# Down projections of a macaron block: 16 of 22 blocks by seven half-size products, weight sums by adding DMAs

## The chip, the cores and the metric

The kernel runs on one core of one Trainium2 chip. Times are device microseconds of one execution, the median of several runs. The core has a tensor engine (PE, whose weight loads are shown apart as PEld), a vector engine (DVE), a scalar engine (ACT), GpSimd (POOL) and a sync engine (SP). DMAs are issued from queues; in this kernel weights are loaded from SP's queue, and POOL's queue carries gains and some constants.

## The reference, cut to what matters

One layer of a hybrid block on 512 tokens with 1024 channels: a half-step SwiGLU FFN, a token mixer (attention and mLSTM), and a second half-step FFN. The change touches the down projections of the two FFNs only.

```python
D_MODEL, SEQ = 1024, 512
D_FF = ((8 * D_MODEL // 3 + 127) // 128) * 128      # 2816, 22 blocks of 128

def swiglu(x, w_gate, w_up, w_down):
    return (jax.nn.silu(x @ w_gate) * (x @ w_up)) @ w_down

f = swiglu(rmsnorm(x, ffn1_pre_g[l]), ffn1_w_gate[l], ffn1_w_up[l], ffn1_w_down[l])
x = x + 0.5 * rmsnorm(f, ffn1_post_g[l])
...
f = swiglu(rmsnorm(x, ffn2_pre_g[l]), ffn2_w_gate[l], ffn2_w_up[l], ffn2_w_down[l])
x = x + 0.5 * rmsnorm(f, ffn2_post_g[l])
```

All is in float32.

## The kernel before

**Arithmetic.** Each float32 operand is split in a high part (a cast to float32r on ACT) and a low part (the difference, on DVE). A product is three passes: high x high, low x high, high x low. So every weight block and every activation block needs a cast on ACT and a subtraction on DVE (called a low) before PE can use it.

**The down projection** is (512 tokens x 2816) x (2816 x 1024). Its result stands in all eight PSUM banks: `accs[t][b]`, four token tiles t by two column halves b. A *plain* block is one 128-row slice of the weights: 4 x 2 x 3 = 24 matmuls of 128x512 in `step` (L230). Of the 22 blocks, 12 go by seven half-size products (the Winograd form of Strassen's scheme): tokens, rows and columns are halved, and seven products of a quarter of the size do the work of eight. Class `Down` does this. Its rows are cut in three thirds g = 0, 1, 2 of two blocks in each half, and `STEPS` lists the steps as product and third: "20" is product 2 of third 0. One step is 12 matmuls (`product`, L510). Products 1, 2, 3 take a weight block as it lies; 5, 6, 7, 4 take sums of weight blocks, and 5, 6, 7, 3 take sums of activation blocks. Steps p and q are plain blocks (`FILL`), p for the first half of the tokens and q for the second, put in where others need time. `middle` combines accumulators once a product's last third is done.

**How a step is made ready.** `fetch` issues its load on SP into one of six buffers (`room`: three of tag "wf", three of tag "bf"); `sums` makes the sums on DVE, weights into T (in the place of the FFN's input hTh) and activations into S (in the place of hTl); `cast` runs on ACT, `low` on DVE. In the loop of `run`, with step n on PE, loads go out 5 steps ahead, sums and casts 2 ahead, lows 1 ahead. All instructions of this part go through `Order` (`do`), which keeps each engine to the order of the calls, so the order in `run` is the order in the queues of PE, ACT, DVE, SP and POOL.

**Around it.** The first steps are prepared and begun inside the last unit of the gate and up projections (`seven`, a generator `ahead` that is advanced there). After the steps, `down` does the remaining plain blocks 15 to 21: three of them at once, the last four (`KEEP`) held, so that the banks end one after the other and `PostNorm` can take them up. `late` adds an accumulator that is left over. `load_gains` issues two gain rows (second FFN: one) from POOL's queue at the start of the stage.

Of the kernel before, what the change touches and what calls it, by code (L numbers as in the profile page):

```python
# [16 lines left out]
P = 128  # L17
T = 512
# [21 lines left out]
def tile_hybrid_block(ctx: ExitStack, tc: tile.TileContext, a: dict):  # L40
# [42 lines left out]
    def load_w(src, name, n=1024, after=()):  # L83
        wf = act.tile([P, WMAX], F32, tag="wf", bufs=3, name=f"wf_{name}")[:, :n]
        nc.sync.dma_start(wf, src)
        with ExitStack() as st:
            for i in after:
                st.enter_context(tc.issue_after(i))
            wh = wpool.tile([P, WMAX], F32R, tag="wh", bufs=5, name=f"wh_{name}")[:, :n]
            nc.scalar.copy(wh, wf)  # L90
            wl = wpool.tile([P, WMAX], F32R, tag="wl", bufs=5, name=f"wl_{name}")[:, :n]
            nc.vector.tensor_tensor(wl, wf, wh.bitcast(F32), op=ALU.subtract)  # L92
        return wh, wl
# [58 lines left out]
    class PostNorm:  # L152
        def __init__(self, t, g, where, name, half=False):
            self.t, self.g, self.name, self.half = t, g, f"p{name}{t}", half
            self.fg = scratch(f"fg_{name}{t}", *where)
            self.ss = small.tile([P, 2], F32, tag="sp", name=f"sp_{name}{t}")

        def bank(self, acc, b):
# [3 lines left out]
            nc.vector.tensor_tensor(self.fg[:, BANKS[b]], acc[b], self.g[:, BANKS[b]], op=ALU.mult)  # L162
# [37 lines left out]
    def down(n, chunk_src, get_x, post, finish, todo, name, accs=None, first=0, late=lambda: None):  # L200
        pins = []
        held = []
        accs = accs or [pair(f"acc_{name}{t}") for t in range(NT)]
        for kk in range(first, n):
            xh, xl = get_x(kk)
            wh, wl = load_w(chunk_src(kk), f"{name}d{kk}")
            if kk < n - KEEP:
                for t in range(NT):
                    for b in range(2):
                        step(accs[t][b], xh, xl, wh, wl, t, b, kk == 0, False)  # L210
                    if kk == first and t == 1:
                        late()
# [71 lines left out]
    def seven(do, fs, wgu, x, low, scr, aT, name, ahead):  # L284
# [76 lines left out]
        for i in range(len(fs)):  # L361
# [33 lines left out]
            if w:  # L395
# [8 lines left out]
    HALF = 6  # L404
    FILL = (12, 13, 14)
    STEPS = "20 21 10 50 60 11 51 61 12 52 62 22 p0 p1 70 30 p2 71 31 72 32 40 41 42 q0 q1 q2".split()
    LOADS = {"1": ((0, 0),), "2": ((1, 0),), "5": ((0, 1),), "6": ((1, 1),), "7": ((0, 0),), "3": ((1, 1),),
             "4": ((1, 0),)}
# [4 lines left out]
    class Down:  # L413
        after = FILL[-1] + 1

        def __init__(self, do, wdq, wd, aT, scr, name):
            self.do, self.wdq, self.wd, self.aT, self.scr, self.name = do, wdq, wd, aT, scr, name
            self.xp, self.src, self.x, self.w, self.wf = None, {}, {}, {}, {}
            self.accs = [[None, None] for _ in range(NT)]
            self.n = 0  # L420

        def tt(self, out, p, q, op):
            self.do("vector", "tensor_tensor", out, p, q, op=op)

# [7 lines left out]

        def room(self, n):
# [5 lines left out]
        def fetch(self, s):  # L439
            if s[0] in "pq":  # L440
                t = self.room(f"B{s}_{self.name}").rearrange("p a b -> p (a b)")
                self.do("sync", "dma_start", t, self.wd[FILL[int(s[1])]])
                self.src[s] = self.aT[:, FILL[int(s[1])], None, slice(0, H) if s[0] == "p" else slice(H, T)], halves(t, T)
            for k, j in LOADS.get(s[0], ()):
                t = self.room(f"B{k}{j}_{self.name}{s}")
                self.do("sync", "dma_start", t, halves(self.wdq[int(s[1]), k, j], T))
                self.wf[s[1], k, j] = t

        def sums(self, s, early=False):
            k, g = s[0], int(s[1])  # L450
            if k in "pq":
                return
            A, B = (lambda i, j: self.A(i, j, g)), (lambda i, j: self.wf[s[1], i, j])
            x = A(*{"1": (0, 0), "2": (0, 1), "4": (1, 1)}.get(k, (0, 0)))
            w = B(*{"1": (0, 0), "2": (1, 0), "3": (1, 1)}[k]) if k in "123" else None
            if k in "64":
                w = self.T[:, 2 * g:2 * g + 2, :]
            if early:
                w = self.scr.tile([P, 2, Q], F32, tag="cd", bufs=1, name=f"t1_{self.name}")
                x = self.scr.tile([P, 2, Q], F32, tag="ab", bufs=1, name=f"s1_{self.name}")[:, :, :H]  # L460
            elif k in "57":
                x, w = halves(self.S[:, 7, :], H), self.T[:, 6:8, :]
            if k == "5":
                self.t1, self.s1 = w, x
                self.tt(w, B(0, 1), B(0, 0), SUB)
                self.tt(x, A(1, 0), A(1, 1), ADD)
            elif k == "6":
                x = halves(self.S[:, g, :], H)
                self.tt(w, B(1, 1), self.t1, SUB)
                self.tt(x, self.s1, A(0, 0), SUB)  # L470
            elif k == "7":
                self.tt(w, self.T[:, 2 * g:2 * g + 2, :], B(0, 0), SUB)
                self.tt(x, A(0, 0), A(1, 0), SUB)
            elif k == "3":
                x = work.tile([P, 2, H], F32, tag="s4", bufs=1, name=f"s4_{self.name}{g}")
                self.tt(x, A(0, 1), halves(self.S[:, g, :], H), SUB)
            elif k == "4":
                self.tt(w, B(1, 0), w, SUB)
            self.src[s] = x, w

        def cast(self, s, which):
# [4 lines left out]
            self.do("scalar", "copy", halves(hl[0], v.shape[2]), v)  # L486
            (self.w if which == "w" else self.x)[s] = hl

        def low(self, s, which):
            v = self.src[s][which == "w"]  # L490
            h, l = (halves(y, v.shape[2]) for y in (self.w if which == "w" else self.x)[s])
            self.tt(l, v, h.bitcast(F32), SUB)
# [20 lines left out]
        def middle(self, s):  # L513
            q1, p5 = self.S[:, 3:5, :], self.S[:, 5:7, :]
            for i in range(2):
                if s == "12":
                    self.do("scalar", "copy", q1[:, i, :], self.out["1"][i])
                elif s == "52":
                    self.do("scalar", "copy", p5[:, i, :], self.out["5"][i])
                elif s == "62":  # L520
                    self.tt(self.out["6"][i], self.out["6"][i], q1[:, i, :], ADD)
                elif s == "72":
                    self.tt(self.out["1"][i], self.out["7"][i], p5[:, i, :], ADD)
            if s == "62":
# [3 lines left out]
        def late(self):  # L528
            for i in range(2):
                self.tt(self.out["2"][i], self.out["2"][i], self.S[:, 3 + i, :], ADD)  # L530

        def run(self):
            s0, s1, s2, s3, s4 = STEPS[:5]
            self.fetch(s0)
# [4 lines left out]
            self.fetch(s1)  # L539
            self.fetch(s2)  # L540
            self.fetch(s3)
# [3 lines left out]
            self.sums(s3, True)  # L545
# [10 lines left out]
            self.fetch(s4)  # L556
            self.cast(s3, "w")
            yield
            self.cast(s3, "x")
            self.low(s3, "w")  # L560
            self.low(s3, "x")
            self.product(s1)
            self.sums(s4)
            yield
            self.fetch(STEPS[5])
            for x in "wx":
                self.cast(s4, x)
            self.product(s2)
            self.fetch(STEPS[6])
            self.fetch(STEPS[7])  # L570
            for n in range(3, len(STEPS)):
                if n + 5 < len(STEPS):
                    self.fetch(STEPS[n + 5])
                if n + 2 < len(STEPS):
                    self.sums(STEPS[n + 2])
                    for x in "wx":
                        self.cast(STEPS[n + 2], x)
                if n + 1 < len(STEPS):
                    for x in "wx":
                        self.low(STEPS[n + 1], x)  # L580
# [3 lines left out]
    def ffn(pool, todo, first_w, hT, wgu, wdq, wd, post, finish, name, begin=None, pins=(), aT=None):  # L584
# [54 lines left out]
        pins = down(NF, lambda kk: wd[kk], get_x, post, finish, todo, name, d.accs, d.after, d.late)  # L639
# [4 lines left out]
    with new_pool("ffn_a") as fa:  # L644
# [112 lines left out]
        def post1(t):  # L757
            if t == 2:
                hT.extend(new_hT("mx"))
            return PostNorm(t, gains[0], tbuf[t % 2], "f1", True)  # L760
# [640 lines left out]
    with new_pool("ffn_b") as fb:  # L1401
        def post3(t):
            return PostNorm(t, g_post2[0], [(work, "tmp"), (work, "tmp2")][t % 2], "f2", True)
# [43 lines left out]
def _layout(inp):  # L1447
# [11 lines left out]
    for i, n in ((1, "ffn1"), (2, "ffn2")):  # L1459
# [3 lines left out]
        r[f"wdq{i}"] = wd[:12].reshape(2, 3, 2, P, 2, 512).transpose(1, 0, 4, 3, 2, 5).reshape(3, 2, 2, P, 1024)  # L1463
# [51 lines left out]
```

## Time and profile before

| | |
|---|---|
| median of 3 runs | 1348.43 us (1348.35 to 1348.59) |
| the profiled execution | 1348.25 us |
| its span, first to last instruction | 1346.4 us |
| DVE busy | 998.9 us |
| ACT busy | 627.4 us |
| granted TensorE clock | 0.999 |

The first down projection stands at about 238 to 347 us, the second at about 1224 to 1340. A name such as `wh_a` ends in the FFN (a or b); B is a loaded weight block, T and S the sums, `acca` to `accd` pairs of banks, and wh/wl, xh/xl the high and low parts. A row of a timeline has the start, the length, engine, line, operation, output <- inputs, and how many are merged; in square brackets the idle time before it and who ended it. A row of the DMA issues has a count, the size and the median time to landing. A window row has the stretch, its length, and the busy time of PE, PEld, DVE, ACT and POOL with the number of instructions, then the granted clock, the share of the DMA engines, and GB/s.

### The profile page before, as it was taken

The numbers are of one execution on the slowest core, as the hardware profiler recorded it, in microseconds if no ns is written. First come the engines' busy times: TensorE is split into PE (matmuls) and PEld (weight loads), VectorE is DVE, ScalarE is ACT, GpSimd is POOL, SyncE is SP. The second block draws the span as 40 slices with busy tenths as digits, with TensorE's granted clock in tenths as the row PEclk, the third lists the DMA queues.
The fourth block names the chain that finished last, engine by engine and source line by source line (L and its number), as shares of the span: only waits on it lengthen the run. The fifth ranks groups of instructions, "written<-read, shape, count | busy, mean of one in ns | idle before, by whom it ended". The sixth has DMA issues, their size and how long they took to land.

```text
span 1346.4 us, 20568 instructions
## 1 busy us (share of the span) xinstructions
PE 1336.1 (99%) x8247; PEld 1200.1 (89%) x8247; DVE 998.9 (74%) x1511; ACT 627.4 (47%) x1010; POOL 37.1 (3%) x64
## 2 busy tenths in 40 slices
PE   9999999999999999999999999999999999999998
PEld 8899999878998888888888889999888999998786
DVE  7799898996755557475756776766379798997983
ACT  5444444555643544534544444344264444444552
POOL 1000000000300000000000000000010000000000
PEclk9999999999999999999999999999999999999999
DMA  5333333654333422422222212335313233335441
GB/s 197 95 101 110 108 97 110 234 174 152 128 101 122 141 79 94 152 68 78 80 78 78 78 48 78 103 102 196 133 57 102 94 110 108 97 110 202 172 143 62
DMA packets 42719, 153.95 MB, mean 114 GB/s; under 512 B 4836, under 2 KB 4844, under 8 KB 42368
## 3 DMA queue, kind: packets, MB, share of 16 engines
q1 hardware_dynamic: 39456, 140.56, 31.5%
q0 software_dynamic: 3152, 12.08, 2.7%
q8 instruction: 64, 1.05, 0.3%
q14 instruction: 31, 0.25, 0.1%
q10 hardware_dynamic: 16, 0.00, 0.0%
HBM read 146.33 MB, written 6.29 MB: 113 GB/s over the span
## 4 chain that ended last, share of the span: by engine, by line
PE 89%; DVE 7%; issue 2%; ACT 1%; DMA 1%; DVEq 0%; SPq 0%; POOLq 0%; POOL 0%; ACTq 0%
PE qb_b L325 9%; PE qb_a L325 9%; PE pq L175 8%; PE pm L175 6%; PE p L175 6%; PE qa_a L325 4%; PE qa_b L325 4%; PE qb_gm L1073 4%; PE acc_o L230 3%; PE pvo L1199 2%; PE pvo L1201 2%; PE pvo L1200 2%; PE pq L189 2%; PE pg_b L189 2%; PE pg_b L175 2%
## 5 line engine op out<-in xcount | busy, mean ns | idle before, releaser
L175 PE MATMUL pq<-hTh_mx,wh_qk 128*128 128x512 f32 x160 | 63.2, 395 | 0.0
L175 PE MATMUL pq<-hTl_mx,wh_qk 128*128 128x512 f32 x160 | 62.4, 390 | 0.0
L92 DVE TENSOR_TENSOR wl_qk<-wf_qk,wh_qk 128x1024 fp32r<-128x1024 f32 x24 | 29.4, 1223 | 33.4 <-ACT wh_qk L90 16.7
L175 PE MATMUL pm<-hTh_mx,wh_mqk 128*128 128x512 f32 x128 | 50.3, 393 | 0.0
L1199 PE MATMUL pvo<-wh_vo,hTh_mx 128*128 128x512 f32 x128 | 50.3, 393 | 0.0
L175 PE MATMUL pm<-hTl_mx,wh_mqk 128*128 128x512 f32 x128 | 49.9, 390 | 0.0
L1201 PE MATMUL pvo<-wl_vo,hTh_mx 128*128 128x512 f32 x128 | 49.9, 390 | 0.0
L1200 PE MATMUL pvo<-wh_vo,hTl_mx 128*128 128x512 f32 x128 | 49.8, 389 | 0.0
L92 DVE TENSOR_TENSOR wl_mqk<-wf_mqk,wh_mqk 128x1024 fp32r<-128x1024 f32 x16 | 19.6, 1225 | 35.1 <-ACT wh_mqk L90 26.1
L90 ACT CAST wh_qk<-wf_qk 128x1024 fp32r<-128x1024 f32 x24 | 25.0, 1045 | 43.0 <-issue 11.6
L175 PE MATMUL pq<-hTh_mx,wl_qk 128*128 128x512 f32 x160 | 39.6, 390 | 0.0
L250 ACT CAST wh_a<-cd_a 128x1024 fp32r<-128x1024 f32 x18 | 18.9, 1050 | 40.2 <-DVE cd_a L250 40.2
L250 ACT CAST wh_b<-cd_b 128x1024 fp32r<-128x1024 f32 x18 | 18.9, 1049 | 38.6 <-DVE cd_b L250 38.6
L994 DVE SCALAR_TENSOR_TENSOR z<-pm,cw,z 128x511 f32<-128x511 f32 (+2 forms) x48 | 35.3, 745 | 1.4 <-ACT z L992 0.9
L325 PE MATMUL qa_a<-hTl_f,wh_a 128*128 128x256 f32 x144 | 36.1, 283 | 0.0
L325 PE MATMUL qa_a<-hTh_f,wh_a 128*128 128x256 f32 x144 | 36.1, 283 | 0.0
L325 PE MATMUL qa_b<-hTl_f,wh_b 128*128 128x256 f32 x144 | 36.1, 283 | 0.0
L325 PE MATMUL qa_b<-hTh_f,wh_b 128*128 128x256 f32 x144 | 36.1, 283 | 0.0
L90 ACT CAST wh_mqk<-wf_mqk 128x1024 fp32r<-128x1024 f32 x16 | 16.8, 1049 | 40.7 <-PE pvo L1200 22.3
L175 PEld LDWEIGHTS pq<-hTh_mx,wl_qk 128*128 128x128 f32 x160 | 30.0, 188 | 6.2
L175 PEld LDWEIGHTS pq<-hTh_mx,wh_qk 128*128 128x128 f32 x160 | 30.1, 188 | 6.0
L175 PEld LDWEIGHTS pq<-hTl_mx,wh_qk 128*128 128x128 f32 x160 | 30.1, 188 | 6.0
(746 smaller groups left out, 4532.9 us busy)
## 6 DMA issues: line engine op xcount, KB each, us to landing
wf_qk<-in_wqk SPq DMA_DIRECT2D x24, 512.0 KB, 3.3
B_a<-in_wdq SPq DMA_DIRECT2D x21, 512.0 KB, 3.7
B_b<-in_wdq SPq DMA_DIRECT2D x21, 512.0 KB, 3.4
g_a<-in_wgu SPq DMA_DIRECT2D x18, 512.0 KB, 3.8
u_a<-in_wgu SPq DMA_DIRECT2D x18, 512.0 KB, 3.7
g_b<-in_wgu SPq DMA_DIRECT2D x18, 512.0 KB, 3.7
u_b<-in_wgu SPq DMA_DIRECT2D x18, 512.0 KB, 3.7
wf_mqk<-in_wmqk SPq DMA_DIRECT2D x16, 512.0 KB, 3.3
```

The lines of the kernel that those rows point to most:

```text
L90: nc.scalar.copy(wh, wf)
L92: nc.vector.tensor_tensor(wl, wf, wh.bitcast(F32), op=ALU.subtract)
L175: nc.tensor.matmul(out, lhsT=wt[:, k * P:(k + 1) * P], rhs=x[:, k, 0:T], start=n == 0, stop=n == len(terms) - 1)
L189: nc.tensor.matmul(outs[b][:, tok], lhsT=ws_[b][w][:, k * P:(k + 1) * P], rhs=x[:, k, tok], start=i + k + hf == 0, stop=hf == 1 and i == 2 ...
L230: nc.tensor.matmul(out, lhsT=x[:, tk], rhs=w[:, cs], start=first and n == 0, stop=last and n == 2, skip_group_check=True)
L250: self.last[eng] = getattr(getattr(nc, eng), fn)(*args, **kw).ins
L325: nc.tensor.matmul(out, lhsT=wt[:, i * P:(i + 1) * P], rhs=y[:, i, :], start=first and n == 0, stop=last and n == len(terms) - 1, skip_gro ...
L994: nc.vector.scalar_tensor_tensor(z[:, s:], src[:, :T - s], cw[:, ct, 3 - s:4 - s], z[:, s:], op0=ALU.mult, op1=ALU.add)
L1073: nc.tensor.matmul(out, lhsT=wt[:, i * P:(i + 1) * P], rhs=y[:, i, :], start=first and m == 0, stop=last and m == len(terms) - 1, skip_gro ...
L1199: nc.tensor.matmul(out, lhsT=hTh[:, k, tk], rhs=wh[:, cs], start=k == 0, stop=False)
L1200: nc.tensor.matmul(out, lhsT=hTl[:, k, tk], rhs=wh[:, cs], start=False, stop=False)
L1201: nc.tensor.matmul(out, lhsT=hTh[:, k, tk], rhs=wl[:, cs], start=False, stop=k == KD - 1)
```

## The change

The 22 blocks are now 16 by seven products (four groups g = 0 to 3 of two blocks in each half, so `HALF` is 8 and there are 28 such steps), 2 plain blocks as p and q steps, and 4 plain blocks at the end, all of them held; the three unheld ones and `late` are gone (the leftover addition is made in `middle` after step 41).

The signs of the scheme are turned so that every sum of weight blocks is a plain addition. The second column half of the result comes out negated: plain blocks take that half of their weights with a minus (`flip` in `cast_w` and `load_w`, and the same in `cast` and `low` for p and q), and `PostNorm` turns it back.

The sums of weights are no longer made on DVE. For group g, `chain` loads block (0,0) into T from SP's queue and adds block (0,1) by a DMA with `accum_op` from POOL's queue: the weights of product 5. When the low of 5 has been taken, a DMA adds block (1,1) (product 6), and when the low of 6 has been taken, one adds block (1,0) (product 4). `pairs` makes (0,1) + (1,1) in a buffer u3 of its own (product 7). Loads go out 7 steps ahead, sums and casts 3, lows 2.

```diff
+    def cast_w(wh, wf, flip=False):
+        if not flip:
+            return nc.scalar.copy(wh, wf)
+        nc.scalar.copy(wh[:, :T], wf[:, :T])
+        return nc.scalar.mul(wh[:, T:], wf[:, T:], -1.0)
...
+            m = T if flip else n
+            nc.vector.tensor_tensor(wl[:, :m], wf[:, :m], wh[:, :m].bitcast(F32), op=ALU.subtract)
+            if flip:
+                nc.vector.scalar_tensor_tensor(wl[:, T:], wf[:, T:], -1.0, wh[:, T:].bitcast(F32), op0=ALU.mult,
+                                               op1=ALU.subtract)
...
-            nc.vector.tensor_tensor(self.fg[:, BANKS[b]], acc[b], self.g[:, BANKS[b]], op=ALU.mult)
+            if b and self.flip:
+                nc.vector.scalar_tensor_tensor(self.fg[:, BANKS[b]], acc[b], -1.0, self.g[:, BANKS[b]], op0=ALU.mult,
+                                               op1=ALU.mult)
+            else:
+                nc.vector.tensor_tensor(self.fg[:, BANKS[b]], acc[b], self.g[:, BANKS[b]], op=ALU.mult)
...
-    HALF = 6
-    FILL = (12, 13, 14)
-    STEPS = "20 21 10 50 60 11 51 61 12 52 62 22 p0 p1 70 30 p2 71 31 72 32 40 41 42 q0 q1 q2".split()
+    HALF = 8
+    FILL = (16, 17)
+    STEPS = ("20 21 22 10 11 12 50 51 52 53 13 60 61 62 63 23 p0 70 30 71 31 72 32 73 33 p1 "
+             "40 41 42 43 q0 q1").split()
+    RAW = {"1": (0, 0), "2": (1, 0), "3": (1, 1)}
+    CHAIN = {"5": (0, 1), "6": (1, 1), "4": (1, 0)}
...
+        def add(self, out, g, k):
+            self.do("gpsimd", "dma_start", out, self.B(g, CHAIN[k]), accum_op=ADD)
+
+        def chain(self, g):
+            self.do("sync", "dma_start", self.U(g), self.B(g, RAW["1"]))
+            self.add(self.U(g), g, "5")
+
+        def pairs(self, g):
+            t = self.u3[g] = work.tile([P, D], F32, tag=TEMPS[g], bufs=1, name=f"u3_{self.name}{g}")
+            t = halves(t, T)
+            self.do("sync", "dma_start", t, self.B(g, CHAIN["5"]))
+            self.add(t, g, "6")
...
+            if which == "w" and s[0] in "56":
+                self.add(self.U(int(s[1])), int(s[1]), "6" if s[0] == "5" else "4")
...
             for n in range(3, len(STEPS)):
-                if n + 5 < len(STEPS):
-                    self.fetch(STEPS[n + 5])
-                if n + 2 < len(STEPS):
-                    self.sums(STEPS[n + 2])
-                    for x in "wx":
-                        self.cast(STEPS[n + 2], x)
-                if n + 1 < len(STEPS):
-                    for x in "wx":
-                        self.low(STEPS[n + 1], x)
+                lead = 2 if n < 5 else 3
+                self.fetch(n + 7)
+                if n < 7:
+                    self.pairs(n - 3)
+                self.front(n + lead)
+                self.back(n + lead - 1)
                 self.product(STEPS[n])
                 self.middle(STEPS[n])
```

How the instructions stand, in three places. First POOL's queue at the start of the first down projection and up to the mixer's first rows, before:

```order
L97 DMA g_f1post<-in_ffn_post_g 128x1024
L97 DMA g_mpre<-in_mix_pre_g 128x1024
L1149 DMA selr<-in_sel 4x512
L104 TENSOR_TENSOR r_pf_3696<-v_pf_3694,nhalf 128x1
L1102 DMA xkeep_3932<-x_86 128x1024
```

and now (the DMAs into T_a and u_a are the adding ones; u_a is u3):

```order
L263 DMA T_a<-in_wdq 128x1024
L107 DMA g_f1post<-in_ffn_post_g 128x1024
L107 DMA g_mpre<-in_mix_pre_g 128x1024
L263 DMA T_a<-in_wdq 128x1024 x3
L263 DMA u_a_2982<-in_wdq 128x1024
L263 DMA u_a_3005<-in_wdq 128x1024
L263 DMA u_a_3029<-in_wdq 128x1024
L263 DMA T_a<-in_wdq 128x1024 x2
L263 DMA u_a_3064<-in_wdq 128x1024
L263 DMA T_a<-in_wdq 128x1024 x6
L1196 DMA selr<-in_sel 4x512
```

Sixteen DMAs have come into this queue. The first four into T are the adds for product 5, the next four (two, then two after u_a_3064) those for 6, the last four those for 4; three adds into u3 stand ahead of the first add for 6.

Second, SP's queue in the same stretch, with buffer numbers, now:

```order
L263 DMA B10_a_2902<-in_wdq1 128x1024
L263 DMA T_a_2900<-in_wdq1 128x1024
L263 DMA B11_a_2944<-in_wdq1 128x1024
L263 DMA T_a_2900<-in_wdq1 128x1024
L263 DMA B12_a_2956<-in_wdq1 128x1024
L263 DMA T_a_2900<-in_wdq1 128x1024 x2
L263 DMA B13_a_2980<-in_wdq1 128x1024
L263 DMA u3_a0_2982<-in_wdq1 128x1024
L263 DMA u3_a1_3005<-in_wdq1 128x1024
L263 DMA u3_a2_3029<-in_wdq1 128x1024
L263 DMA u3_a3_3064<-in_wdq1 128x1024
L263 DMA B23_a_3110<-in_wdq1 128x1024
```

Before, only loads of whole blocks (B, Bp, Bq) stood here. The first loads into T and into u3 have come in between, eight of them, all ahead of B23.

Third, DVE around products 5 and 6, before:

```order
L250 TENSOR_TENSOR T_a<-B_a_3004,B_a_2982 128x1024
L250 TENSOR_TENSOR S_a<-aT_a 128x512
L250 TENSOR_TENSOR wl_a<-B_a_2982,wh_a 128x1024
L250 TENSOR_TENSOR xl_a<-aT_a,xh_a 128x512
L250 TENSOR_TENSOR T_a<-B_a_3028,T_a 128x1024
L250 TENSOR_TENSOR S_a<-S_a,aT_a 128x512
L250 TENSOR_TENSOR wl_a<-T_a,wh_a 128x1024
L250 TENSOR_TENSOR xl_a<-S_a,xh_a 128x512
```

and now:

```order
L263 SCALAR_TENSOR_TENSOR S_a<-S_a,aT_a 128x512
L263 TENSOR_TENSOR wl_a<-T_a,wh_a 128x1024
L263 TENSOR_TENSOR xl_a<-S_a,xh_a 128x512
L263 SCALAR_TENSOR_TENSOR S_a<-S_a,aT_a 128x512
L263 TENSOR_TENSOR wl_a<-T_a,wh_a 128x1024
L263 TENSOR_TENSOR xl_a<-S_a,xh_a 128x512
```

The 1024-wide sums into T are gone from DVE; the 512-wide sums into S and the lows stay.

157 lines of the change are left out of this document (85 added, 72 removed).

## The prediction

> **What bounds the kernel now.** I read the page first (busy shares, chain), then PE's timeline over the down projections, then who waits for whom there, then DVE, ACT and the DMA windows of that stretch.
>
> ```profile
> span 1346.4 us, 20568 instructions
> PE 1336.1 (99%) x8247; PEld 1200.1 (89%) x8247; DVE 998.9 (74%) x1511; ACT 627.4 (47%) x1010; POOL 37.1 (3%) x64
> PE 89%; DVE 7%; issue 2%; ACT 1%; DMA 1%; DVEq 0%; SPq 0%; POOLq 0%; POOL 0%; ACTq 0%
> ```
>
> PE is busy all the time and carries 89% of the chain, so time is won by removing matmuls, or by closing gaps between them, and lost by opening gaps. The timeline of PE at the first down projection gives the pace:
>
> ```profile
> 237.53 0.64 PE L325 MATMUL qb_a<-hTh_f,wl_a 128*128 128x256 f32 x4
> 242.19 1.09 PE L510 MATMUL acca_a<-wh_a,xh_a 128*128 128x512 f32 x4
> 244.94 1.07 PE L510 MATMUL accd_a<-wh_a,xh_a 128*128 128x512 f32 x4
> 247.66 1.07 PE L510 MATMUL accc_a<-wh_a,xh_a 128*128 128x512 f32 x4
> 257.42 0.50 PE L510 MATMUL accb_a<-wh_a,xh_a 128*128 128x512 f32 x1 [0.38 <-ACT xh_a L250]
> 299.91 1.19 PE L510 MATMUL accb_a<-wl_a,xh_a 128*128 128x512 f32 x4 [0.28 <-DVE wl_a L250]
> 315.61 0.39 PE L230 MATMUL acca_a<-wh_ad,ah_a 128*128 128x512 f32 x1
> ...
> 1228.36 1.09 PE L510 MATMUL acca_b<-wh_b,xh_b 128*128 128x512 f32 x4
> 1301.76 0.39 PE L230 MATMUL acca_b<-wh_bd,ah_b 128*128 128x512 f32 x1
> ```
>
> One step of 12 matmuls takes 2.72 us (244.94 to 247.66), 0.227 us a matmul. Between 242.19 and 315.61 stand the steps from 21 to q2, 26 of them: 26 x 2.72 = 70.72, but 73.42 passed. So PE **lost 2.70 us** there, and by 1228.36 and 1301.76 (73.40) 2.68 us in the second FFN. Who holds PE up:
>
> ```profile
> ACT wh_a L250 <- DVE T_a L250: 23.6, 10, 4.0
> 254.48 1.22 DVE L250 TENSOR_TENSOR T_a<-B_a,T_a 128x1024 f32<-128x1024 f32 x1
> 255.62 0.69 DVE L250 TENSOR_TENSOR S_a<-S_a,aT_a 128x512 f32<-128x512 f32 x1
> 256.22 1.22 DVE L250 TENSOR_TENSOR wl_a<-T_a,wh_a 128x1024 fp32r<-128x1024 f32 x1
> 257.35 0.69 DVE L250 TENSOR_TENSOR xl_a<-S_a,xh_a 128x512 fp32r<-128x512 f32 x1
> 257.95 1.23 DVE L250 TENSOR_TENSOR wl_a<-T_a,wh_a 128x1024 fp32r<-128x1024 f32 x1
> 255.79 1.05 ACT L250 CAST wh_a<-T_a 128x1024 fp32r<-128x1024 f32 x1 [1.88 <-DVE T_a L250]
> 256.75 0.62 ACT L250 CAST xh_a<-S_a 128x512 fp32r<-128x512 f32 x1
> 280.00:300.00 20.00, 19.72 (x88) 16.02 (x86) 19.96 (x25) 9.56 (x14) 0.00 (x0) 1.00 0.60 217
> ```
>
> In the window row DVE (fourth figure, 19.96 of 20 us) is full. From start to start a 1024-wide operation costs it 1.14 or 1.13 us, a 512-wide one 0.60. A step with sums needs both lows and both sums, 3.5 us, against 2.72 of PE. ACT waits 23.6 us for weight sums (T), and PE waits behind ACT: the gaps are DVE's.
>
> **The change part by part.**
> *Matmuls.* Of the 22 blocks 12 became 252 matmuls and 10 plain ones 240, 492 in all. Now 16 become 28 steps x 12 = 336, and 6 plain ones 144: 480. That is 12 fewer in each FFN, 2 x 12 x 0.227 = **-5.44 us**, all on the bound engine.
>
> *DVE.* The four weight sums of a third (5, 6, 7, 4: 4 x 1.13 us) leave DVE. A seven-product step now asks 1.13 + 0.60 for lows and at most one 0.60 activation sum, 2.33 us against 2.72. The sums in the accumulators after 63, 73 and 41 have one to three steps of cover, as they had. So the old gaps can go: **-2.70 and -2.68 us**. With the product count that makes -10.82 us, if nothing else becomes late.
>
> *The sums as DMAs.* Here is the price. In each FFN 16 adding DMAs of 512 KB go through POOL's queue. SP's plain loads fall from 34 to 28, but 8 of these (four into T, four into u3) are new and stand early. The trace has no adding DMA. It does show what plain transfers take:
>
> ```profile
> 248.00:250.00 2.00, 2.00 (x11) 1.65 (x10) 1.40 (x3) 1.82 (x3) 0.00 (x0) 1.00 1.02 412
> 292.00:294.00 2.00, 2.00 (x10) 1.68 (x9) 2.00 (x3) 0.49 (x1) 0.00 (x0) 1.00 1.02 408
> 240.00:260.00 20.00, 19.62 (x92) 15.95 (x91) 18.12 (x24) 11.52 (x16) 1.26 (x2) 1.00 0.83 302
> wf_ad<-in_wd SPq DMA_DIRECT2D x7, 512.0 KB, 3.3
> g_f1post<-in_ffn_post_g POOLq DMA_DIRECT2D x1, 512.0 KB, 6.3
> 242.66 0.71 POOL L97 DMA_DIRECT2D g_f1post<-in_ffn_post_g  x1 [224.09 <-PE qb_a L325]
> 245.76 0.55 POOL L97 DMA_DIRECT2D g_mpre<-in_mix_pre_g  x1 [2.39 <-DVE aT_a L250]
> ```
>
> The last two figures of a window are the share of the DMA engines and GB/s. At a share of 1.02 they moved 412 GB/s: 524,288 B take 1.27 us, and this stretch already stood at 0.83. An adding DMA moves the same bytes in, so it costs at least **1.27 us** of the engines; it must also fetch what it adds to, and if both streams pass one after the other it costs **2.54**. No row is nearer to one end, so I take the middle, **1.91 us**, and keep both.
>
> Now the deadline. Step 60 is the twelfth; at full pace it starts at 244.94 + 9 x 2.72 = 269.4, and its two casts (255.79 to 257.37, 1.58 us) must start at 267.8. They need the second add into T, which POOL issues after ten others in its queue: four first adds, two gains, three adds into u3 and itself. Those wait in turn for loads on SP's queue. T takes hTh's place, so its first load starts when PE has read hTh, at 238.2 (237.53 + 0.64). It lands 3.3 us later at 241.5; B11 and the second T load bring the clock to 244.0. From there the engines are never short of work until the add for 60 has landed:
> - two gains, 2 x 1.27 = 2.54;
> - eight adds, 8 x 1.91 = 15.28;
> - eight loads that stand ahead on SP (B12, two T, B13, four u3), 10.16; with B23 and Bp0 behind them, which share the engines, ten, 12.70.
>
> It lands at 272.0 to 274.5, **4.2 to 6.7 us late**. From 60 to 63 four more adds (51, u3, 52, 53) take 7.64 us, with four loads beside them 12.72, against 8.16 us of PE: 0 to 4.6 more. Together 4.2 to 11.3, middle 7.8 us. The second FFN loads one gain less (1.27): middle 6.5. What is queued behind: ACT takes its casts in order, so a late T holds all later casts, and PE with them. The adds for 4 (needed fifteen steps after 60) and for 7 (u3, needed at step 70) have time.
>
> Sum: -10.82 + 7.8 + 6.5 = **+3.5 us**. The profiled execution took 1348.25 us (span 1346.4 and 1.85 around it), 0.18 under the median: 1351.7 there, **1352** for the median.
>
> The Trainium skill's "Collectives: The Full Stack" (section "The bandwidth ceiling: the fold count and why AG ≠ RS ≠ AR") speaks against the change. It says that a DMA that adds is slowed not by the addition but by its two source reads, which queue on the same read ring, so it runs at half the rate of a copy. Its figure, about 31 GB/s an engine halved, over 16 engines, would give as an estimate 2.11 us for an add, and the same sum would then end at 1356. No run so far shows an add; the rule is a rival below, priced from rows.
>
> *Edits at nothing.* Signs are turned by two half casts and two half lows in place of one (0.52 more on ACT at most, 0.07 on DVE, both with room), in PostNorm by a scalar_tensor_tensor in place of a tensor_tensor of equal width. Lows two steps ahead fit: five buffers each for w and x. At the end the four held blocks no longer have three plain blocks as cover. The last of them needs the place of q0, so it can be cast 2.72 us before the held matmuls begin and is used 9 matmuls (2.0 us) into them; 1.05 + 1.22 + 0.62 us of work fit into 4.7. If its load is late this opens a gap of 0 to 1 us in each FFN; I take 0.
>
> **The rivals.**
> *Adds at a copy's price, gaps gone (ends faster).* At 1.27 us the add for 60 lands at 266.9 to 269.4, 0 to 1.6 us late; the next four need 5.1 to 10.2 against 8.16: in all 0 to 3.6, second FFN 0 to 2.3. Middle: -10.82 + 1.8 + 1.2 = -7.8, **1340.5**; at best 1337.5. For it: both old causes of waiting are gone. Against: the stretch would have to run at 400 GB/s from 238 on without a hole, and 240 to 260 held 302. The side turns at the price p of an add where 24p - 32.2 (both FFNs, middle counts) equals 10.8, at **1.79 us**; above it, as in my forecast, the kernel is slower.
> *Two passes.* At 2.54 us it lands at 277.0 to 279.6, 9.2 to 11.8 late, and 2.0 to 7.1 follow: 15.0 and 13.8 in the middle, +18.0, **1366**, at most 1374. This is what that rule of the Trainium skill would make of it.
> *Adds far slower, or run one at a time with their latency* (6.3 us from issue to landing for POOL's gain): 12 adds from 242 to the last one for 63 would take 76 us where 34 are there, over 1400.
>
> **How the numbers follow.** The forecast (an add between 1.6 and 2.2 us) 0.37; copy price 0.36; two passes 0.20; far slower 0.07. About 0.2% (2.7 us) is what a measurement here can tell from no change; stalls summing to 8.1 to 13.5 us stand for that, p from 1.68 to 1.90. The forecast's case thus gives 0.02 to faster, 0.14 to the same and 0.21 to slower; with the others faster 0.38, same 0.14, slower 0.48. The forecast's own range is 1344 (both low counts) to 1359; for 8 in 10 it goes from 1339 (into the copy case) to 1375 (the end of two passes).
>
> **What would show it.** PE should have 24 matmuls fewer; DVE's 1024-wide sums should be gone and its share near 0.85 or less in that stretch; ACT's longest waits should be for T from a DMA, not from DVE. Time from issue to landing of T's adds tells the price. A gap before 60 and 62 in PE's timeline with DMA share near 1.0 from 240 to 275 confirms the forecast; no gap there and 1340 refutes the deadline sum; gaps before 50 to 53 would mean that single adds are slow. I am wrong too if POOL's issue itself is long, or if the held blocks wait.

## The result, and the profile after

The changed kernel takes **1384.45 us** (median of 4 runs, 1383.94 to 1384.99) where the kernel before took 1348.39 us (1348.13 to 1348.59, 4 runs beside them): a ratio of 1.0267 (1.0255 to 1.028). The prediction was 1352, with a range of 1339 to 1375. It had the side that it held likelier, and by far not the size: 36 us slower, not 3.5. The profiled execution took 1384.99 us.

The page of the changed kernel: span, busy shares, the granted clock over the 40 slices, and the shares of the chain that ended last.

```profile
span 1383.2 us, 20639 instructions
PE 1339.1 (97%) x8223; PEld 1202.1 (87%) x8223; DVE 987.1 (71%) x1519; ACT 637.7 (46%) x1034; POOL 65.3 (5%) x96
...
PEclk9999999979999999999999999999999999999899
...
PE 90%; DMA 7%; DVE 1%; issue 1%; ACT 1%; POOL 0%; SPq 0%; POOLq 0%; DVEq 0%; ACTq 0%
```

Two numbers say what became of the change. The 24 matmuls are gone (8247 before, 8223 now), and DVE's 7% of the chain has become 1%; but DMA, 1% before, now holds 7%. PE's busy time rose by 3 us although it does less, and the clock row has a dip in the ninth slice and a smaller one near the end, where before it had none. The view of what PE waited for, with the total, the number of waits and the longest (the lines of the two down projections):

```profile
PE accb_a L547 <- ACT xh_a L263: 13.8, 2, 9.9
PE accb_b L547 <- ACT xh_b L263: 12.5, 2, 10.5
PE accc_a L547 <- ACT xh_a L263: 4.9, 2, 4.4
PE accc_b L547 <- ACT xh_b L263: 3.2, 3, 1.6
```

`accc` is product 5's bank, `accb` product 6's. The gaps sum to 18.7 us in the first FFN and 15.7 in the second. The timeline of PE shows where they stand and what comes behind them (start, length, and in brackets the idle time and who ended it):

```profile
263.72 2.07 PE L547 MATMUL accc_a<-wh_a,xh_a 128*128 128x512 f32 x4 [4.44 <-ACT xh_a L263]
265.59 1.65 PE L547 MATMUL accc_a<-wl_a,xh_a 128*128 128x512 f32 x4
...
287.08 2.08 PE L547 MATMUL accb_a<-wh_a,xh_a 128*128 128x512 f32 x4 [9.94 <-ACT xh_a L263]
...
298.32 2.07 PE L547 MATMUL accb_a<-wh_a,xh_a 128*128 128x512 f32 x4 [3.83 <-ACT xh_a L263]
```

The gaps stand before steps 51, 60 and 62. Behind each of them four matmuls take 1.87 us from start to start (263.72 to 265.59) where 0.91 is the pace: PE is not only late, it also starts again at half speed. The windows bear on both (the last three figures are the granted clock, the share of the DMA engines, GB/s):

```profile
240.00:260.00 20.00, 19.28 (x91) 15.87 (x89) 12.57 (x16) 8.18 (x12) 4.80 (x6) 1.00 0.99 317
244.00:285.00 41.00, 28.23 (x116) 22.23 (x114) 18.43 (x23) 10.90 (x14) 11.19 (x14) 0.90 1.05 298
...
280.00:300.00 20.00, 9.09 (x28) 7.03 (x29) 6.68 (x8) 7.40 (x11) 2.45 (x3) 0.68 1.06 251
282.00:284.00 2.00, 0.00 (x0) 0.00 (x0) 0.00 (x0) 0.00 (x0) 0.00 (x0) 0.50 1.05 270
308.00:352.00 44.00, 44.00 (x195) 36.42 (x194) 39.99 (x57) 27.62 (x42) 0.00 (x0) 1.00 0.30 94
```

From 244 to 285 the DMA engines were never free (1.05), and yet they moved 298 GB/s, not the 412 that the prediction had read from the kernel before. Between 282 and 284 no engine did anything but the DMA engines. From 308 to 352 PE has no gap and the full clock. What stood in the queue ahead of the add for step 60 shows in POOL's timeline, and the landing of that add in ACT's:

```profile
261.40 0.87 POOL L263 DMA_DIRECT2D u_a<-in_wdq  x1 [5.47 <-DMA u_a<-in_wdq]
264.94 0.87 POOL L263 DMA_DIRECT2D u_a<-in_wdq  x1 [2.67 <-DMA u_a<-in_wdq]
268.99 0.87 POOL L263 DMA_DIRECT2D u_a<-in_wdq  x1 [3.18 <-DMA u_a<-in_wdq]
269.54 2.12 POOL L263 DMA_DIRECT2D T_a<-in_wdq  x2
...
285.47 1.05 ACT L263 CAST wh_a<-T_a 128x1024 fp32r<-128x1024 f32 x1 [12.68 <-DMA T_a<-in_wdq]
```

POOL issues in order. The add for 60 is the first of the two at 269.54; it had to wait behind three adds into u3 (`u_a`), each of which waited for its plain load. It landed at 285.4, and ACT's cast, which stands before all later casts, began then. The prediction had the landing at 272.0 to 274.5, so the place and the kind of the wait were right and the size was not.

How much of the longer stage is gap, and how much clock? In the first FFN the down stage went from 238.01 to 355.27 before, 117.26 us (it ends at 355, not at the 347 given ahead of the prediction):

```profile
238.01 1.09 PE L510 MATMUL acca_a<-wh_a,xh_a 128*128 128x512 f32 x4
...
355.27 0.39 PE L230 MATMUL accd_a<-wl_ad,ah_a 128*128 128x512 f32 x1
```

Now it goes from 238.59 to 376.26, 137.67 us:

```profile
238.59 1.09 PE L547 MATMUL acca_a<-wh_a,xh_a 128*128 128x512 f32 x4
...
376.26 0.39 PE L243 MATMUL accd_a<-wl_ad,ah_a 128*128 128x512 f32 x1
```

With 2.72 us of matmuls and the old gaps of 2.70 us gone it should take 111.84. The difference of 25.8 us is 18.7 of gaps and, as the rest, 7.1 of slow matmuls and restarts behind them. This says where the time stands, not yet what each part costs; the clock has a run of its own below.

### The profile page after: what moved, and what is told of

Same layout as the page of the kernel before. It is cut to its first block, busy times and chain, and to the rows that moved or that the text cites. A ratio compares the mean times of both kernels' runs of the same rounds, so it can differ in the third digit from the quotient of the medians.

```text
span 1383.2 us, 20639 instructions
## 1 busy us (share of the span) xinstructions
PE 1339.1 (97%) x8223; PEld 1202.1 (87%) x8223; DVE 987.1 (71%) x1519; ACT 637.7 (46%) x1034; POOL 65.3 (5%) x96
## 3 DMA queue, kind: packets, MB, share of 16 engines
q8 instruction: 64, 1.05, 0.3%
## 4 chain that ended last, share of the span: by engine, by line
PE 90%; DMA 7%; DVE 1%; issue 1%; ACT 1%; POOL 0%; SPq 0%; POOLq 0%; DVEq 0%; ACTq 0%
PE qb_b L338 9%; PE qb_a L338 9%; PE pq L189 8%; PE pm L189 6%; PE p L189 6%; PE qa_b L338 4%; PE qa_a L338 4%; PE qb_gm L1120 4%; PE acc_o L243 3%; PE accb_a L547 2%; PE pvo L1246 2%; PE pvo L1248 2%; PE pvo L1247 2%; PE accb_b L547 2%; DMA T_a<-in_wdq 2%; PE pq L203 2%
## 5 line engine op out<-in xcount | busy, mean ns | idle before, releaser
L263 DVE TENSOR_TENSOR wl_a<-T_a,wh_a 128x1024 fp32r<-128x1024 f32 x12 | 14.7, 1224 | 30.2 <-ACT wh_a L263 30.2
```

Source lines behind the costliest of these rows:

```text
L263: self.last[eng] = getattr(getattr(nc, eng), fn)(*args, **kw).ins
```

## The experiments

Theory 1: an adding DMA takes the DMA engines about twice as long as a copy, they are full, and so the sums are late. Theory 2: it is the queue of POOL, its latency and its order of issue, whatever the transfers do. Beside them two questions: does the amount of transfers count or their order, and does the slow clock cost something of its own?

### Copies in place of the adds

```diff
-            self.do("gpsimd", "dma_start", out, self.B(g, CHAIN[k]), accum_op=ADD)
+            self.do("gpsimd", "dma_start", out, self.B(g, CHAIN[k]))
```

> All 16 adding DMAs of each FFN become plain copies of the same bytes from the same queue, so the weight sums of the products 5, 6, 4 and 7 are wrong. Theory 1 (an add costs the 16 DMA engines about 2.6 us, twice a copy, and the engines are full from 244 to 308 us): 16 x 1.3 us of demand go in each FFN, the gap before step 60 falls from 9.9 us to 2 at most, the granted clock stays at 1.00, and the time is 1337 to 1345 us. Theory 2 (POOL's queue carries one transfer after the other with its latency, whatever the transfer does): the gaps stay, 1370 us or more.

Measured: 1356.11 us (one run), between the theories. The price alone is worth 28.3 us, and still the kernel stayed behind the one before. A window and a row of PE of this run:

```profile
244.00:276.00 32.00, 28.06 (x116) 22.36 (x114) 18.39 (x23) 10.87 (x14) 7.07 (x14) 0.95 1.03 405
```

```profile
278.10 2.08 PE L547 MATMUL accb_a<-wh_a,xh_a 128*128 128x512 f32 x4 [4.12 <-ACT xh_a L263]
```

This is the run that showed the second error. With every transfer at a copy's price the engines were full until 276 us, at 405 GB/s, and step 60 was still 4.1 us late. 405 GB/s for 32 us are 24.7 transfers of 524,288 B. The prediction had counted 18 to 20 ahead of that add (two gains, eight adds, eight to ten loads). SP's timeline of the changed kernel has the loads that were not counted:

```profile
254.85 19.91 SPq L263 DMA_DIRECT2D B_a<-in_wdq  x4
```

By their place in SP's queue these are the four plain loads for steps 30 to 33, the first issued at 254.85 us and the last at about 274.4, all before the add for 60 had landed.

### Product 7's transfers later, with adds and with copies

```diff
-                if n < 7:
-                    self.pairs(n - 3)
+                if 7 < n < 12:
+                    self.pairs(n - 8)
```

> The four loads and four adds for the weight sums of product 7 are issued from steps 8 to 11 on and no longer from steps 3 to 6; nothing else changes. Theory 1, by deadlines (what counts is how much stands in the queues ahead of the add for step 60): three adds of 2.6 us and three or four loads of 1.27 us, 12 to 13 us, are no longer ahead of it; the gap before 60 goes from 9.9 us to below 2, a smaller one of up to 5 us can open before 70 to 73; 1345 to 1360 us. Rival, by volume (the engines have 65 us of work up to the last sum that is needed, in whatever order): the gap only moves from 60 to 70, 1375 us or more.

Measured: 1354.28 us (1354.14 to 1354.53), 1.0044 (1.0029 to 1.0059) of before. What moved is smaller than the expectation says. On SP's queue nothing holds a load back until its step, and u3's four loads still left between 243.8 and 252.9 us; only u3's adds on POOL's queue moved, behind the first adds for product 6. A row of SP and two of POOL:

```profile
245.40 1.89 SPq L263 DMA_DIRECT2D u_a<-in_wdq  x2
```

```profile
254.60 0.86 POOL L263 DMA_DIRECT2D T_a<-in_wdq  x1 [0.60 <-DVE wl_a L263]
...
271.49 2.12 POOL L263 DMA_DIRECT2D u_a<-in_wdq  x2
```

The add for step 60 was issued at 254.60 us, in place of 269.54, and ACT's cast behind it began at 272.2 in place of 285.5. So the order of POOL's queue, a part of theory 2, had held this add back by 15 us. What PE waited for:

```profile
PE accc_a L547 <- ACT xh_a L263: 3.7, 1, 3.7
PE accc_b L547 <- ACT xh_b L263: 3.2, 3, 1.6
PE accb_a L547 <- ACT xh_a L263: 1.7, 2, 1.0
PE accb_b L547 <- ACT xh_b L263: 1.8, 2, 1.0
```

The waits before product 6 fell from 26.3 us to 3.5 and did not come back at product 7: 30.2 us are a matter of the order in POOL's queue. The waits before product 5 (4.9 and 3.2, now 3.7 and 3.2) hardly changed, since nothing that stands ahead of the first adds was moved. Both edits at once:

> Both edits at once: plain copies in place of the adds (weight sums wrong) and the transfers for product 7 from steps 8 to 11 on. If late sums and the clock after their gaps are all that the change costs, and the matmuls and DVE's gaps are worth the 10.8 us of the prediction: 1337 to 1341 us. Well above 1341 with no gap before 50 to 73 would mean that something else was added, the held blocks or the flipped casts.

Measured: 1342.20 us (one run, with wrong sums as in the run with copies), 1.2 above the upper bound that I had set; what is over is one gap of 2.0 us in the first FFN and the slow matmuls behind it. The four runs make a square: adds with u3 early 1384.45, copies early 1356.11, adds late 1354.28, copies late 1342.20. The price is worth 28.3 us in the old order and 12.1 in the new one; the order 30.2 with adds and 13.9 with copies. Neither is the cause by itself; as I read it, lateness is what is left when the work ahead exceeds the time up to the deadline.

### The price by itself

A program of its own issues transfers of 512 KB, plain loads from SP and POOL and adds from POOL, and nothing else.

> Not the kernel: 512 KB transfers by themselves, in phases. Eight plain loads on SP's queue, eight plain loads on POOL's, eight adds into eight tiles on POOL's, four adds one after another into one tile, and eight adds beside eight plain loads. Theory 1: 1.27 to 1.35 us for a plain load from either queue, 2.5 to 2.7 us for an add into a tile of its own with the DMA share near 1, so eight adds take 20 to 22 us beside 10 to 11 for eight loads. Theory 2: plain loads on POOL's queue are already slower than SP's, and eight adds into eight tiles take as long each as the four dependent ones. Between 1.6 and 2.2 us for an independent add would mean that my 1.91 was right and the loss is elsewhere.

The phases did not stay apart: each tile went on as soon as its own transfer had landed, so loads and adds overlap, and the comparison of dependent with independent adds that I had meant to make is not to be had from it. But there is a stretch in which only loads move, and one in which only adds do (here the columns are DVE and POOL, then as above):

```profile
7.00:12.00 5.00, 0.31 (x2) 0.53 (x1) 1.00 1.03 403
...
46.00:55.00 9.00, 1.14 (x8) 0.00 (x0) 1.00 1.07 211
```

At a full share the engines carry 403 GB/s of loads and 211 GB/s of adds, counted by the bytes that come in: 1.30 us and **2.48 us** for 524,288 B. My middle of 1.91 is refuted, and the price was close to the upper bound, 2.54. With theory 1 this fits the changed kernel: 298 GB/s for 41 us are 23.3 transfers; with 8 adds at 2.48 and 15.3 copies at 1.27 they take 39.3 us of those 41.

The Trainium skill, in "Collectives: The Full Stack", section "The bandwidth ceiling: the fold count and why AG ≠ RS ≠ AR", gives a reason for such a ratio: of the reducing step of a collective it says that the add needs two source reads on the same ring, and so runs at half the rate of the copying one. The ratio here agrees: 211 to 403 GB/s is 1.91. Where in the engines the second stream queues, no run here shows. The estimate of 2.11 us that the prediction worked out from that page of the Trainium skill was too low, since its 31 GB/s an engine would be 496 over 16, and plain loads reach 403 to 412 here.

### The loads that run ahead

Two runs ask whether plain loads delay the sums.

```diff
-            if self.xp and self.n % 2:
+            if self.xp:
```

> The raw B blocks of the down stage rotate through three buffers and no longer through six, so SP can run three loads less far ahead. In the traces of the changed kernel and of the copy run some fifteen loads stood ahead of or beside the add for step 60, where my prediction counted eight to ten; the four loads for 30 to 33 are the difference. If these loads share the engines at the cost of the sums: three of them, 3.8 us, go from ahead of step 60 in each FFN, 1374 to 1379 us. If only the adds and the u loads count: 1384, or more where a plain block is then late.

Measured: 1383.02 us (one run), against my expectation. SP's timeline of this run says why:

```profile
237.95 0.33 SPq L91 DMA_DIRECT2D wf_ad<-in_wd  x1
...
259.10 0.33 SPq L91 DMA_DIRECT2D wf_ad<-in_wd  x1
```

The three buffers that I had taken from the rotation were free now, and the loads of the held plain blocks (`wf_ad`), which in the changed kernel are issued from 322.6 us on, moved up into them: one at 237.95 us, a second at 242.13, a third at 259.10. They stood where the loads for 30 to 33 had stood, which now left from 276 us on. Nearly as many loads ran ahead as before; the run tells nothing on the question. The second one moves the loads themselves:

```diff
-                    self.do("sync", "dma_start", t, self.B(int(s[1]), RAW[s[0]]))
+                    self.do("gpsimd" if s[0] == "3" else "sync", "dma_start", t, self.B(int(s[1]), RAW[s[0]]))
```

> The changed kernel, with the four plain loads for steps 30 to 33 issued from POOL's queue, where they stand behind the adds for 60 to 63, and no longer from SP's, where they run ahead as soon as a buffer is free. By the new count (the engines are full from 244 us on, and everything that is issued before the add for 60 delays it): these four loads, 4 x 1.27 = 5.1 us, go from ahead of the add; the gap before 60 falls by about 5 us in each FFN: 1373 to 1377 us. If the loads on SP's queue do not delay POOL's: 1384.

Measured: 1370.65 us (one run), 13.8 us less, somewhat more than expected. The add for step 60 landed 3.6 us earlier (285.47 before, now 281.86), 0.8 of it because this run's stage began earlier (237.81 where it was 238.59):

```profile
281.86 1.04 ACT L263 CAST wh_a<-T_a 128x1024 fp32r<-128x1024 f32 x1 [10.72 <-DMA T_a<-in_wdq]
...
284.34 1.05 ACT L263 CAST wh_a<-T_a 128x1024 fp32r<-128x1024 f32 x1 [0.92 <-DMA T_a<-in_wdq]
```

So loads on SP's queue that nobody needs yet take engine time from adds on POOL's. The two landings stand 2.48 us apart, which is the price again, inside the kernel. That the time fell by more than the landing moved is because the gap before 62 went too, in both FFNs (3.83 and 1.95 us in the changed kernel), and in the first the slow matmuls behind it.

### The clock

```diff
+            for _ in range(ZEROS[self.name].get(s, 0)):
+                nc.tensor.matmul(self.out["2"][0], lhsT=self.z[:, :P], rhs=self.z, start=False, stop=False,
+                                 skip_group_check=True)
```

> Products with zeros are added in the accumulators ahead of steps 51 (17 matmuls, first FFN), 60 (40, both) and 62 (24 and 12), 133 matmuls or 30 us of PE that stand in the gaps and change no sum. If the slow clock after a gap costs time of its own on the way to the end: the matmuls after the gaps run at 0.227 us each, and the time falls. By deadlines only the slow steps after the last gap count (62 and 63 of the first FFN took 8.36 us where 5.44 is the pace, 2.9 us; in the second FFN a gap follows the slow steps and takes them in, 0 to 1): 1380 to 1383 us. If every slow step counts (about 11 us in all): 1372 to 1375. If the clock has no part in it, the filler only fills: 1384 to 1387.

Measured: 1383.00 us (1381.77 to 1383.08), 1.0255 (1.0237 to 1.0272) of before. With 30 us of matmuls more, the kernel is not slower and perhaps 1.4 us faster. The fillers and what follows them in the first FFN, and a window:

```profile
283.65 1.52 PE L559 MATMUL acca_a<-z_a 128*128 128x512 f32 x6
286.33 1.20 PE L548 MATMUL accb_a<-wh_a,xh_a 128*128 128x512 f32 x4 [1.16 <-ACT xh_a L263]
```

```profile
280.00:300.00 20.00, 18.02 (x78) 14.20 (x77) 8.17 (x10) 9.13 (x14) 2.62 (x3) 1.00 1.06 250
```

The clock stayed at 1.00 where it had been 0.68 on the mean, the matmuls ran at the pace, and next to nothing was won. This fits the account by deadlines: slow matmuls ahead of a further gap cost nothing, because PE would have waited there anyway, and only those behind the last gap count. The down stage of the first FFN shrank from 137.67 to 135.16 us, 2.5, and the second did not (130.31 and 131.02).

### A better order, and the first sums back on DVE

The next run is to put the transfers in the order of their deadlines. Its edit also sets SP's loads back from 7 steps ahead to 5:

```diff
-    STEPS = ("20 21 22 10 11 12 50 51 52 53 13 60 61 62 63 23 p0 70 30 71 31 72 32 73 33 p1 "
+    STEPS = ("20 21 22 10 11 12 13 50 51 52 53 60 61 62 63 23 p0 30 31 32 33 70 71 72 73 p1 "
...
-                self.fetch(n + 7)
-                if n < 7:
-                    self.pairs(n - 3)
+                self.fetch(n + 5)
+                if n == 14 and self.begin:
+                    self.begin()
+                if 9 < n < 14:
+                    self.pairs(n - 10)
+                if 15 < n < 20:
+                    self.add(self.U(n - 16), n - 16, "4")
```

> The changed kernel with its transfers in the order in which they are due: product 3 before product 7, 13 before 50, the loads and adds for product 7 issued from steps 10 to 13, the third adds into T (for product 4) from steps 16 to 19, the gains at step 14 in place of before the stage. The sums are still made by adding DMAs. With 2.5 us an add and 1.27 us a load, from 241.5 us: three loads into T, six B loads and four first adds end near 263, the add for step 60 at 266 to 268, where 267.8 is its deadline. If the order in the queues is the cause of the loss: 1338 to 1345 us, faster than before. If the volume is: the engines have 54 us of work up to step 73 in any order and gaps of over 3 us appear before 60 to 73: 1350 us or more.

Measured: 1354.46 us (1353.96 to 1356.86), 1.005 (1.0033 to 1.0067): no better than moving u3's adds alone. The time is in the range of the rival by volume, but the gaps of over 3 us before 60 to 73 that it named did not appear; the longest is 2.4 us, ahead of them. Nor did the edit bring the whole order about: u3's four loads still left SP between 243.8 and 257.1 us. So this run does not decide between order and volume. The waits of PE in it, and one of ACT's in the first FFN:

```profile
PE accb_b L547 <- ACT xh_b L263: 3.7, 4, 1.4
PE accb_a L547 <- ACT xh_a L263: 2.8, 4, 1.6
PE accd_a L547 <- ACT xh_a L263: 2.4, 1, 2.4
PE accd_b L547 <- ACT xh_b L263: 1.3, 1, 1.3
...
ACT wh_a L263 <- DMA B_a<-in_wdq: 10.7, 3, 7.2
```

Now a raw block of product 1 (`accd`), that of step 13, is late instead: ACT waited 7.2 us for its load, which had left SP at 242.3 and shared the engines with the sums and with u3's loads until 257.1. The gains had not moved either: they were still issued at 244 us. Holding them back behind the adds, on top of this order:

> The reordered kernel with all sixteen adds, and the gains held back behind the adds for 60 to 63 as in the kernel with DVE's four sums: what stands between the two is now the four first sums alone. Two gains of 1.25 us go from ahead of the sums in the first FFN, one in the second: 1350 to 1354 us, still slower than before, if the four first sums (10 us of engine time in each FFN) are what counts. If the gains were the decisive part: 1345 or less.

Measured: 1352.49 us (1349.76 to 1353.76, 10 runs), 1.0028 (1.0018 to 1.0038). Worth some 2 us, as expected. If what is left is engine time, it must help to take work off the engines, and the next edit does only that: T is loaded with B12, and DVE adds the block B11 that product 1 has loaded anyway.

```diff
-            self.do("sync", "dma_start", self.U(g), self.B(g, RAW["1"]))
-            self.add(self.U(g), g, "5")
+            self.do("sync", "dma_start", self.U(g), self.B(g, CHAIN["5"]))
...
+            if which == "w" and s in SUM5:
+                for g in SUM5[s]:
+                    self.tt(self.U(g), self.U(g), self.wf[f"1{g}"], ADD)
```

> The reordered kernel of the run before, but the four first sums (B11 + B12 for product 5) are made by DVE: T is loaded with B12, and DVE adds the raw B11 block that product 1 has loaded for itself, 4 x 1.14 us of DVE in each FFN in place of 4 adds of 2.5 us on the DMA engines; the gains are held back on POOL's queue behind the adds for step 60 to 63. Twelve adds stay DMAs. If the engines' time ahead of step 60 is the cause: 17 to 20 us of transfers stand ahead of the add for 60 from 241.5 us, it lands near 262, before its deadline, no gap over 1 us opens, and the time is 1338 to 1343 us, faster than before. Rival: DVE, which waits in order for the loads into T, now holds the lows back; gaps of 1 to 3 us before 21 to 13 and 1345 to 1352 us.

Measured: **1337.88 us** (1337.62 to 1338.24), 0.9922 (0.9906 to 0.9939) of before: 10.6 us faster than the kernel before and 46.6 faster than the changed one. Its page, and two windows:

```profile
PE 1327.6 (99%) x8223; PEld 1197.1 (90%) x8223; DVE 995.0 (74%) x1527; ACT 636.3 (48%) x1034; POOL 58.2 (4%) x88
...
PE 99%; DVE 0%; ACT 0%; issue 0%; DVEq 0%; POOLq 0%; POOL 0%; ACTq 0%
```

```profile
240.00:260.00 20.00, 20.00 (x96) 16.78 (x95) 19.47 (x23) 12.22 (x17) 1.04 (x1) 1.00 0.99 387
260.00:280.00 20.00, 20.00 (x90) 16.57 (x89) 17.68 (x24) 13.87 (x22) 10.47 (x13) 1.00 1.06 234
```

PE has no gap in either window and carries 99% of the chain. DVE is nearly full from 240 to 260 (19.47 of 20 us, where the changed kernel had 12.57): the sums stand in time in which it had waited. The DMA engines are as full as before (0.99 and 1.06), but the add for step 60 landed in time:

```profile
265.64 1.06 ACT L263 CAST wh_a<-T_a 128x1024 fp32r<-128x1024 f32 x1 [3.33 <-DMA T_a<-in_wdq]
```

That is later than the expected 262 and before the deadline of 267.8. Against the run before, the four sums are the only difference, and they are worth 14.6 us. Last, the same four sums on DVE with the rest of the change left as it was, except that step 13 comes before 50:

> The changed kernel with the four first sums made by DVE and step 13 put before 50 (its raw block is needed for the last of them); product 7's transfers, the third adds, the gains and products 7 and 3 stay as the change has them. 10 us of adds go from ahead of the add for step 60 in each FFN: it lands near 275 us, still 7 to 8 us after its deadline, and the slow clock after that gap stays; 1354 to 1364 us. Near 1338 would mean that the order of the rest did not matter.

Measured: 1359.59 us (one run), as expected; the add for 60 landed at 277.2. So the step to 1337.88 needs both: 10 us of adds fewer ahead of step 60 in each FFN, and the rest of the reordering (u3's adds, the third adds and the gains behind those that are due sooner, product 3 before 7, loads 5 steps ahead). Which parts of the rest count in this kernel was not tried one by one.

## Why the prediction was wrong

*Matmuls, -5.44 us, and DVE's gaps, -5.38 us: right.* The count fell by 24, and where no sum is late both show in full: the kernel with DVE's four sums is 10.6 us faster than before, against 10.82 of the prediction. In the run with copies and u3 late the second FFN's down stage went from 115.44 us to 110.06, 5.38 less; 2.72 and 2.68 were foreseen. The kernel with DVE's four sums has the same 110.06 there, and 111.88 in the first FFN in place of 117.26.

*The edits at nothing: right.* Flipped signs, lows two steps ahead and held blocks opened no gap in the kernel that reached 1337.88.

*The deadline: right, with its place.* Step 60 waits for the second add into T, behind ACT's cast, and in the kernel without gaps it starts at 269.42, where 269.4 was foreseen. The predicted sign, a gap before 60 and 62 at a share near 1.0, is there, but it does not tell the sizes apart: with the price and the count both wrong it looks the same. Nor did the time from issue to landing tell the price, as the prediction had hoped: its median for T's adds is 14.1 us, most of it waiting in full engines. (The prediction calls the ten entries of POOL's queue up to this add, itself included, "ten others"; its sum counts them rightly.)

*The price of an add, 1.91 us: the first step that failed.* The bounds were 1.27 and 2.54; the middle between them had no row behind it, and the runs show 2.48. On the eight adds ahead of step 60 this is 4.6 us in each FFN. The rule of the Trainium skill that the prediction quoted spoke for that end and was given 0.20.

*"Eight loads that stand ahead", with two beside them: the second.* The four loads for 30 to 33 were left out. SP issues a load as soon as a buffer is free, not when its step is near, so the later a sum is, the more loads get in beside it. The traces give 23 to 25 transfers ahead of the add where 18 to 20 were counted: 5 x 1.27 = 6.4 us. Four of the five are these loads; the fifth is not identified. With 4.6 for the price, the predicted landing of 272.0 to 274.5 becomes 283 to 285.5; measured 285.4. For the same reason both rivals were too low in their turn: a copy's price was to give 1340.5 and gave 1356.11, two passes were to give 1366, at most 1374.

*Gaps before 50 to 53:* named only as a sign of slow adds; 4.9 and 3.2 us are there, and with copies in place of the adds 1.9 us and none. Of these only what isn't taken in by the later wait for step 60 costs time.

*The clock: not in the prediction.* It costs little here: 1.4 us by the medians, 2.5 by the stage of the first FFN; that this stands behind the last gap there is argued from the rows, not shown by a run of its own. The Trainium skill's "TensorE: Matmul & The Clock Gate", section "Part 1: The HAM clock gate (the "warmup" mystery)", says that TensorE falls to half its clock after an idle window of about 3.4 us. The 0.50 behind the gaps of 4.44, 9.94 and 3.83 us agrees with it. The run with copies and u3 late does not:

```profile
260.69 1.20 PE L547 MATMUL accc_a<-wh_a,xh_a 128*128 128x512 f32 x4 [2.03 <-ACT xh_a L263]
...
263.13 1.91 PE L547 MATMUL accc_a<-wh_a,xl_a 128*128 128x512 f32 x4
```

```profile
262.00:264.00 2.00, 2.00 (x7) 1.51 (x6) 1.84 (x3) 1.22 (x2) 0.21 (x1) 0.52 1.02 408
```

There a gap of 2.03 us was followed by the slow clock, a good microsecond after work had begun again. In the run with zeros a gap of 2.17 us in the second FFN was not: the clock stayed at 1.00 and the matmuls at the pace. So no length of gap can be read from these runs as the limit.

Three things stay open: whether dependent adds cost more than independent ones, since the transfers by themselves did not stay apart; which parts of the reordering are needed beside the four sums; and how the last 2 to 3 us of the reordered kernels divide between the gaps and what follows them.

## What to carry to other kernels

A sum that is moved into a DMA is not free because its engine is idle on the mean: count what the transfers ahead of the first deadline cost, at about twice a copy for every add, and count every load that a free buffer lets run ahead. An in-order queue that feeds a deadline should hold nothing that is due later, and a loader that is not held back by need takes bandwidth from the one that is late. Where an engine and the DMA engines are each full in different stretches, split the sums between them; here four of sixteen on DVE, with the rest of POOL's queue in the order of need, turned 36 us of loss into 10.6 of gain.

## What the hardware showed

- An adding DMA of 512 KB takes the 16 engines 2.48 us at a full share (211 GB/s), a plain one 1.27 to 1.30 (412 and 403 GB/s).
- POOL needs longer to issue an adding one: 0.86 us against 0.53 for a plain load from the same queue, in the run with the transfers by themselves:

```profile
25.38 0.53 POOL L28 DMA_DIRECT2D t<-in_w  x1 [2.03 <-DVE t L21]
...
30.23 0.86 POOL L31 DMA_DIRECT2D t<-in_w  x1 [0.74 <-DVE u L21]
```

- PE at half clock behind a gap need not cost what it seems to: in this kernel 30 us of products with zeros kept the clock at 1.00 (0.68 without them from 280 to 300 us) and changed the time by 1.4 us.
